# Layer norm's two products of ones one column tile earlier, the sum of its squares on VectorE, and a small sum ahead of a weights' product in the last norm

## The chip, the cores and the metric

The kernel runs on one core of a Trainium2 chip. Its time is the device time of one execution in microseconds (us); a kernel is run several times and the median is given. A profiled execution comes with a trace of every instruction of the core's engines: TensorE (PE, with its weight loads PEld), VectorE (DVE), ScalarE (ACT), GpSimd (POOL) and SyncE (SP). SyncE only issues transfers; ScalarE and GpSimd issue some of theirs too.

## The reference

One block of a streaming encoder, for 512 frames of 1024 channels, in float32. Two mixers read the same normalized input and one projection matrix: a gated delta rule with eight heads (with a short convolution of 4 taps, and an output projection `dn_w_o`), and a convolution of 31 taps with a layer norm behind it. Gates merge the two, `w_out` projects, and a SwiGLU layer and a last RMS norm follow. What the change touches is the layer norm and the last norm:

```python
def layernorm(x, w, b):
    mu = jnp.mean(x32, axis=-1, keepdims=True)
    xc = x32 - mu
    y = xc * lax.rsqrt(jnp.mean(xc * xc, axis=-1, keepdims=True) + EPS)
    return y * w + b

c = causal_depthwise_conv(c, cm_dw_w) + cm_dw_b       # 31 taps
c = silu(layernorm(c, cm_ln_w, cm_ln_b))
out_b = c @ cm_w_pw2 + cm_b_pw2
out_a = o @ dn_w_o
x = x + (gate_a * out_a + gate_b * out_b) @ w_out
...
return rmsnorm(x, norm_f_w)                           # last norm
```

## The kernel before

Large products run in three parts, because each float32 operand is split into a high and a low half of a rounded format: high x high, high x low, low x high (`split3`, L115, product at L121). A piece of weights of 128 x 1024 is fetched by SyncE into `raw` (L108); ScalarE makes `whi` from it (L111), VectorE `wlo` = `raw` - `whi` (L112). Three such pieces exist at once, so a piece can be fetched when `wlo` three pieces before is made, and made when TensorE has finished the piece three before.

Activations lie as channels x frames: eight tiles of 128 x 512. A column tile (`col_tile`, L123) is 8 x 3 = 24 products of 128x512 into one bank of PSUM `mm`, of which there are three. The stage that matters here has two loops over eight column tiles:

- The first loop (from L866) multiplies the delta rule's output (`oh`, `ol`, in the trace `yh`, `yl`) with `dn_w_o`. Each tile is multiplied by its gate on VectorE (L875), which frees the bank. The gate is fetched from DRAM into `gsl` (L854), which has two buffers, so gate j + 2 can be fetched when L875 of tile j is done.
- The second loop (from L884) multiplies the layer norm's output, again split into `yh` and `yl` (`split`, L857, ScalarE at L860 and VectorE at L861), with `cm_w_pw2`.

The layer norm lies inside the first loop. The eight convolved tiles are `cv[0]` to `cv[7]`, their sum over tiles is `sacc`. `ln_mean` (L689) sums `sacc` over the partitions by a product with a matrix of ones (L691), scales it to the mean (L693, ScalarE), subtracts it from the eight tiles (L696, VectorE), squares them (L698 and L701, ScalarE) and adds the squares up (L702, GpSimd). `ln_norm` (L705) sums that by a second product of ones (L707), takes the root (L709, ScalarE) and the reciprocal (L710, VectorE), scales the eight tiles (L712, VectorE) and applies weight, bias and SiLU (L713, ScalarE). The two products of ones stand ahead of column tiles 2 and 5 (counted from 0).

Beside this, sums of weights for later stages are made in the background. Each time a piece of weights is fetched, `fill` (L200) may issue a transfer that adds weights in DRAM (`feed_one`, L186: L192 on SyncE, L196 on GpSimd), or load half of a block of `wdn` into `wsh` (`half_load`, L175; the load is L166 on SyncE), or, for a block loaded before, make four adds on GpSimd (L172) and store them to `wsum` (L173, GpSimd's queue) by `dsums_add` (L168). `wsh` has one buffer, so the next load L166 waits for the store L173. While the flag `norming` is set (from the start of this stage to `ln_norm`) no block is loaded or added. `dsums_add` orders its adds behind the instruction kept in `last[0]`.

A scheduler sets each engine's order of instructions from the order in the program and its own estimate; each engine then works through its own list in order, waiting on semaphores of the others.

The last norm works per 128 frames (`squares`, L1156): the squares of a part of a row are summed into `acc` while they are made (ScalarE L1161 or VectorE L1163), a small add (L1164) brings the parts together, GpSimd raises the sum to the power -1/2 (L1166). `weighted` (L1168, through the helper at L1002) multiplies the row by the norm's weight, `scaled` (L1171; L1174 on ScalarE, L1176 on VectorE) applies the root, and the row is stored (L1181). The very last piece of work, the second half of frames 128 to 255, comes in two quarters of 256 columns.

Of the kernel before, what the change touches and what calls it, by code (L numbers as in the profile page):

```python
# [10 lines left out]
ALU = mybir.AluOpType  # L11
# [17 lines left out]
EPS = 1e-6  # L29
# [3 lines left out]
def block_kernel(ctx, tc, a):  # L33
    nc = tc.nc
    V, S, G, PE = nc.vector, nc.scalar, nc.gpsimd, nc.tensor
# [63 lines left out]
    last = [None]  # L99
# [23 lines left out]
    def col_tile(ps, ap, xh, xl):  # L123
        hi, lo = unit(ap)
        for k in range(KD):
            s = slice(k * P, (k + 1) * P)
            split3(ps, (hi[:, s], lo[:, s]), xh[k], xl[k], k == 0, k == KD - 1)
# [14 lines left out]
    cs = []  # L142
# [69 lines left out]
    with tc.tile_pool(name="st", bufs=2) as st:  # L212
# [56 lines left out]
        for k in range(KD):  # L269
# [3 lines left out]
                                   op0=ALU.mult, op1=ALU.subtract)  # L273
            if k % 2 == 0:
                c = slice(k * P, k * P + 256)
# [66 lines left out]
        for k in range(2, 4):  # L342
# [6 lines left out]
                        in1=ss[:, 1].rearrange("p (n a) -> p n a", a=1).broadcast_to([P, NT, 16]), op=ALU.mult)  # L349
# [6 lines left out]
                        in1=rowp[:, 1:2, :].broadcast_to([P, NT, H]), op=ALU.add)  # L356
# [9 lines left out]
        with tc.issue_after(ln_.ins):  # L366
            for g_ in gated:
# [8 lines left out]
                        op=ALU.mult)  # L376
# [312 lines left out]
    def ln_mean():  # L689
        ps = psm.tile([P, T], F32, name="mm")  # L690
        PE.matmul(ps, ones, sacc, start=True, stop=True)  # L691
        mu = tp.tile([P, T], F32, name="pa", bufs=1)
        S.activation(mu, ps, AF.Copy, scale=1.0 / D)  # L693
        vacc = tp.tile([P, T], F32, name="sacc", bufs=1)
        for i in range(KD):
            V.tensor_tensor(out=cv[i], in0=cv[i], in1=mu, op=ALU.subtract)  # L696
            if i == 0:
                S.activation(vacc, cv[i], AF.Square)  # L698
            else:
                sq2 = tp.tile([P, T], F32, name="acc4")  # L700
                S.activation(sq2, cv[i], AF.Square)  # L701
                last[0] = G.tensor_tensor(out=vacc, in0=vacc, in1=sq2, op=ALU.add)  # L702
        return vacc

    def ln_norm(vacc):  # L705
        ps = psm.tile([P, T], F32, name="mm")
        PE.matmul(ps, ones, vacc, start=True, stop=True)  # L707
        rstd = tp.tile([P, T], F32, name="pa", bufs=1)
        S.activation(rstd, ps, AF.Sqrt, scale=1.0 / D, bias=epsc)  # L709
        V.reciprocal(out=rstd, in_=rstd)  # L710
        for i in range(KD):
            V.tensor_tensor(out=cv[i], in0=cv[i], in1=rstd, op=ALU.mult)  # L712
            S.activation(cv[i], cv[i], AF.Silu, scale=ln_w[:, i:i + 1], bias=ln_b[:, i:i + 1])  # L713
# [138 lines left out]
    def gate_of(i):  # L852
        sg = mp.tile([P, T], F32, name="gsl", bufs=2)
        nc.sync.dma_start(sg, sgd[i])  # L854
        return sg
# [8 lines left out]
    mas = []  # L864
    oh, ol = zip(*[split(zall[:, k, :]) for k in range(KD)])
    for j in range(KD):  # L866
        if j == 2:
            vacc = ln_mean()
        if j == 5:
            ln_norm(vacc)  # L870
            norming[0] = False
        ps = psm.tile([P, T], F32, name="mm")
        col_tile(ps, a["wo"][j], oh, ol)
        ma = mp.tile([P, T], F32, name="ma", bufs=KD + 1)
        V.tensor_tensor(out=ma, in0=ps, in1=gate_of(j), op=ALU.mult)  # L875
        mas.append(ma)
# [124 lines left out]
    def tt(out, in0, in1, op, eng=V):  # L1001
        return eng.tensor_tensor(out=out, in0=in0, in1=in1, op=op)  # L1002
# [153 lines left out]
    def squares(hf, n, cs, last=False, eng=S):  # L1156

        sq, acc = dp.tile([P, T], F32, name="rms_sq", bufs=1)[:, 0:cs.stop - cs.start], ss3[:, hf, n:n + 1]
        y, t = y2[:, n, cs], ss3[:, 2, n:n + 1]
        if eng is S:  # L1160
            S.activation(sq, y, AF.Square, scale=1.0 / 32, accum_out=acc)  # L1161
        else:
            V.scalar_tensor_tensor(out=sq, in0=y, scalar=1.0 / D, in1=y, op0=ALU.mult, op1=ALU.mult, accum_out=acc)  # L1163
        V.tensor_scalar(out=t, in0=acc, scalar1=t if hf else EPS, scalar2=None, op0=ALU.add)  # L1164
        if last:
            G.tensor_tensor(out=ss3[:, 3, n:n + 1], in0=t, in1=half, op=ALU.pow)  # L1166

    def weighted(n, cs, eng=G):  # L1168
        tt(ow[n][:, cs], y2[:, n, cs], nfw[:, cs], ALU.mult, eng)
# [8 lines left out]
    def out(n, c):  # L1178
        for cs, eng, q in ((slice(0, c), S, nc.scalar), (slice(c, D), V, nc.sync)):
            scaled(n, cs, eng)  # L1180
            q.dma_start(a["out"][n][:, cs], ow[n][:, cs])  # L1181

    def add(n, cs, what, op=ALU.add, eng=V):
        tt(y2[:, n, cs], y2[:, n, cs], what, op, eng)
# [84 lines left out]
    def part(k, n, ps, c, cw, first, last):  # L1269
        w, x, j = ws[k // 2], set4[k // 2], k % 2  # L1270
        cs, ts = slice(j * T + c, j * T + c + cw), slice(j * TH + n * P, j * TH + n * P + P)
        split3(ps, (w[0][:, cs], w[1][:, cs]), x[0][:, ts], x[1][:, ts], first, last, mv=True)

    K0 = 2 * (len(ws) - 3)
    for k in range(K0):
        for n in range(2):
            part(k, n, p3[n], 0, T, k == 0, n == 1 and k == K0 - 1)
        if k < 2:
            add(2 + k, c1, p4[k])
            squares(0, 2 + k, c1)  # L1280
            squares(1, 2 + k, c2, True)
            weighted(2 + k, c2)
            add(k, c1, p2[k])
            squares(0, k, c1)
        elif k < 4:
            weighted(k, c1)
            for cs, q in ((c2, nc.sync), (c1, nc.scalar)):
                with behind(mybir.EngineType.Activation):
                    scaled(k, cs, S)
                q.dma_start(a["out"][k][:, cs], ow[k][:, cs])  # L1290
            weighted(k - 2, c1, V)
# [6 lines left out]
    for c, b in ((0, bank), (256, bank2)):  # L1298
        ps = b()[:, c:c + 256]
        for k in range(K0, FK):  # L1300
            part(k, 1, ps, c, 256, k == K0, k == FK - 1)
        cs = slice(T + c, T + c + 256)
        if not c:
            out(0, 384)
        add(1, cs, ps)
        squares(4 if c else 1, 1, cs, c, V if c else S)
        weighted(1, cs, V)
    out(1, 384)


# [56 lines left out]
```

## Time and profile before

| | |
|---|---|
| time, median of 3 runs | 957.11 us (956.86 to 957.43) |
| profiled execution | 957.3 us, span of its trace 955.5 us |
| TensorE busy | 942.1 us (99%) |
| VectorE, ScalarE, GpSimd busy | 729.6, 535.3, 350.4 us |
| granted TensorE clock | 0.998 |
| layer norm's products of ones (L691, L707) | start at 482.80 and 500.02 us |
| second loop's first product | 517.28 us |

A row of a timeline gives start and duration in us, engine, line, operation, tiles written and read, count, and in brackets the idle time of the engine just before, with what ended it. Where an instruction waits for several things, the row names the one that came last by the profile; a transfer may have come later. "SPq" is SyncE's queue. A row of waits gives who waited for whom: us in total, times, longest.

### The profile page before, as it was taken

How to read it: one execution, taken by the hardware profiler on the slowest of the kernel's cores; microseconds unless marked ns; L12 is line 12 of the kernel's file. 1: busy time of each engine (PE TensorE's matmuls, PEld its weight loads, DVE VectorE, ACT ScalarE, POOL GpSimd, SP SyncE). 2: the span in 40 equal slices, each digit the busy share in tenths (PEclk: the TensorE clock that was granted, in tenths of full speed). 3: DMA queues.
4: the chain of work that ended last, by engine and by line, in shares of the span. 5: the costliest groups of instructions: out<-in, count | busy, mean ns of one | idle time of the engine just before them, and what ended most of it. 6: DMA issues, size and time to landing. Idle time of an engine off the chain costs nothing.

```text
span 955.5 us, 14889 instructions
## 1 busy us (share of the span) xinstructions
PE 942.1 (99%) x5208; PEld 794.2 (83%) x5208; DVE 729.6 (76%) x1134; ACT 535.3 (56%) x1102; POOL 350.4 (37%) x555
## 2 busy tenths in 40 slices
PE   9999999999999999999999999999999999999997
PEld 6778888887887888888877888888889999988885
DVE  4999887876888888898877753766425887888896
ACT  7697786969756674634546323323324445456545
POOL 1136434344533447444163432254351111133042
PEclk9999999999999999999999999999999999999999
DMA  9234322233232246979887984598899655578654
GB/s 324 104 128 118 102 82 86 92 99 101 70 92 87 89 133 158 316 223 267 273 274 220 315 235 172 181 264 290 277 255 216 198 188 190 177 228 262 210 178 155
DMA packets 78186, 177.39 MB, mean 186 GB/s; under 512 B 10080, under 2 KB 19472, under 8 KB 77088
## 3 DMA queue, kind: packets, MB, share of 16 engines
q1 hardware_dynamic: 66528, 144.89, 45.5%
q0 software_dynamic: 10288, 28.90, 13.4%
q10 hardware_dynamic: 1296, 2.67, 0.7%
q8 instruction: 41, 0.67, 0.3%
q14 instruction: 33, 0.27, 0.1%
HBM read 156.22 MB, written 45.37 MB: 211 GB/s over the span
## 4 chain that ended last, share of the span: by engine, by line
PE 85%; ACT 3%; DVE 3%; issue 2%; DMA 1%; POOL 1%; POOLq 0%; SPq 0%; ACTq 0%; DVEq 0%
PE mm L121 57%; PE w L121 19%; PE g L437 1%; DMA raw<-s 1%; DVE wlo L112 1%; PE st L616 1%; PE st L610 1%; PE b L542 1%; PE g L470 1%; PE b L548 1%; PE b L566 1%; PE st L604 1%; PE g L519 1%; PE st L615 1%; PE st L605 1%
## 5 line engine op out<-in xcount | busy, mean ns | idle before, releaser
L111 ACT ACTIVATE whi<-raw 128x1024 fp32r<-128x1024 f32 (+1 forms) x191 | 196.2, 1029 | 240.7 <-PE mm L121 143.6
L112 DVE TENSOR_TENSOR wlo<-raw,whi 128x1024 fp32r<-128x1024 f32 (+1 forms) x191 | 240.5, 1260 | 88.0 <-ACT whi L111 87.4
L121 PE MATMUL mm<-hh,whi 128*128 128x512 f32 (+1 forms) x688 | 268.9, 391 | 0.3 <-ACT hh L336 0.3
L121 PE MATMUL mm<-hl,whi 128*128 128x512 f32 (+1 forms) x688 | 264.4, 384 | 0.0
L121 PE MATMUL mm<-hh,wlo 128*128 128x512 f32 (+1 forms) x688 | 263.6, 384 | 0.2 <-DVE wlo L112 0.2
L672 DVE SCALAR_TENSOR_TENSOR cps<-c,c31w,cps 128x512 f32<-128x512 f32 x240 | 180.3, 751 | 6.1 <-ACT cps L670 1.8
L121 PEld LDWEIGHTS mm<-hh,wlo 128*128 128x128 f32 x688 | 129.6, 188 | 23.6 <-DVE wlo L112 0.4
L121 PEld LDWEIGHTS mm<-hh,whi 128*128 128x128 f32 x688 | 129.7, 189 | 22.5 <-ACT hh L336 0.8
L121 PEld LDWEIGHTS mm<-hl,whi 128*128 128x128 f32 x688 | 129.9, 189 | 20.8
L1002 POOL TENSOR_TENSOR fm<-fm 128x256 f32<-128x256 f32 x33 | 28.0, 850 | 111.9 <-DVE s L1002 87.4
L424 DVE SCALAR_TENSOR_TENSOR acc<-mm,c4w,acc 128x511 f32<-128x511 f32 (+2 forms) x72 | 53.1, 741 | 6.1 <-ACT acc L421 5.9
L506 POOL TENSOR_TENSOR ytm<-U,y 128x60 f32<-128x60 f32 (+14 forms) x120 | 37.1, 309 | 48.2 <-DMA U<-sc 39.4
L121 PE MATMUL mm<-yl,whi 128*128 128x512 f32 x128 | 50.0, 391 | 2.3 <-DVE yl L861 2.3
L121 PE MATMUL mm<-yh,whi 128*128 128x512 f32 x128 | 50.7, 396 | 0.0
L121 PE MATMUL mm<-yh,wlo 128*128 128x512 f32 x128 | 49.9, 390 | 0.0
L121 PE MATMUL w<-hh,wlo 128*128 128x256 f32 x168 | 47.7, 284 | 0.3 <-DVE wlo L112 0.3
L121 PE MATMUL w<-hh,whi 128*128 128x256 f32 x168 | 47.6, 284 | 0.0
L121 PE MATMUL w<-hl,whi 128*128 128x256 f32 x168 | 47.5, 283 | 0.0
L121 PE MATMUL w<-wlo,fh 128*128 128x512 f32 (+1 forms) x115 | 44.3, 385 | 0.2 <-DVE wlo L112 0.2
L121 PE MATMUL w<-whi,fh 128*128 128x512 f32 (+1 forms) x115 | 44.2, 385 | 0.0
L121 PE MATMUL w<-whi,fl 128*128 128x512 f32 (+1 forms) x115 | 44.2, 384 | 0.0
L196 POOL DMA_DIRECT2D s<-in_wgu_dram x24 | 23.6, 997 | 47.9 <-DMA s<-in_wgu_dram 47.9
(332 smaller groups left out, 1915.8 us busy)
## 6 DMA issues: line engine op xcount, KB each, us to landing
raw<-in_win_dram SPq DMA_DIRECT2D x61, 512.0 KB, 3.5
raw<-in_wgu_dram SPq DMA_DIRECT2D x32, 512.0 KB, 3.6
s<-in_wgu_dram SPq DMA_DIRECT2D x48, 256.0 KB, 5.3
raw<-s SPq DMA_DIRECT2D x48, 256.0 KB, 3.6
raw<-wsum SPq DMA_DIRECT2D x44, 256.0 KB, 3.8
raw<-in_wdn_dram SPq DMA_DIRECT2D x33, 256.0 KB, 3.5
s<-in_wgu_dram POOLq DMA_DIRECT2D x24, 256.0 KB, 7.2
s<-s POOLq DMA_DIRECT2D x24, 256.0 KB, 7.0
```

Source lines behind the costliest of these rows:

```text
L111: marked(S.activation(hi, raw, AF.Copy), "unit")
L112: marked(V.tensor_tensor(out=lo, in0=raw, in1=hi.bitcast(F32), op=ALU.subtract), "unit")
L121: marked(PE.matmul(ps, l, r, start=first and i == 0, stop=last and i == 2))
L196: fed.append(nc.gpsimd.dma_start(*begun.pop(0), accum_op=ALU.add, max_dma_last_dim=2048))
L424: marked(V.scalar_tensor_tensor(out=acc[:, s:], in0=ps[:, :T - s], scalar=c4w[:, j, k:k + 1], in1=acc[:, s:], op0=ALU.mult, op1=ALU.add))
L437: PE.transpose(ps[:, n, :], src[:, n, :], ident)
L470: PE.matmul(ps[:, n, :], kT[:, n, :], kT[:, n, :], start=True, stop=True)
L506: G.tensor_tensor(out=tm[:, :, 0:w], in0=U[:, k, :, k + 1:], in1=y[:, :, k:k + 1].broadcast_to([P, NT, w]), op=ALU.mult)
L519: PE.matmul(ps[:, n, :], kT[:, n, :], qT[:, n, :], start=True, stop=True)
L542: PE.matmul(ps[:, n, 0:16], Ud[:, n, :], xc[:, n, 0:16], start=True, stop=True)
L672: V.scalar_tensor_tensor(out=acc, in0=c[:, k:k + T], scalar=c31w[:, i, k:k + 1], in1=acc, op0=ALU.mult, op1=ALU.add)
L1002: return eng.tensor_tensor(out=out, in0=in0, in1=in1, op=op)
```

## The change

`ln_mean` is called ahead of column tile 1 instead of 2, `ln_norm` ahead of 4 instead of 5. The adds of the squares (L702) go from GpSimd to VectorE, and are no longer kept in `last[0]`. In the last norm `squares` returns its small add, and in the last two quarters `weighted` is issued behind it.

```diff
@@ ln_mean
                 sq2 = tp.tile([P, T], F32, name="acc4")
                 S.activation(sq2, cv[i], AF.Square)
-                last[0] = G.tensor_tensor(out=vacc, in0=vacc, in1=sq2, op=ALU.add)
+                V.tensor_tensor(out=vacc, in0=vacc, in1=sq2, op=ALU.add)
         return vacc
@@ first loop
     for j in range(KD):
-        if j == 2:
+        if j == 1:
             vacc = ln_mean()
-        if j == 5:
+        if j == 4:
             ln_norm(vacc)
             norming[0] = False
@@ squares
-        V.tensor_scalar(out=t, in0=acc, scalar1=t if hf else EPS, scalar2=None, op0=ALU.add)
+        s_ = V.tensor_scalar(out=t, in0=acc, scalar1=t if hf else EPS, scalar2=None, op0=ALU.add)
         if last:
             G.tensor_tensor(out=ss3[:, 3, n:n + 1], in0=t, in1=half, op=ALU.pow)
+        return s_
@@ last two quarters
         add(1, cs, ps)
-        squares(4 if c else 1, 1, cs, c, V if c else S)
-        weighted(1, cs, V)
+        s_ = squares(4 if c else 1, 1, cs, c, V if c else S)
+        with tc.issue_after(s_.ins):
+            weighted(1, cs, V)
```

Behind the diff the lines of the last norm have numbers one to three higher (L1176 becomes L1177).

The scheduler moves more than these lines. First, VectorE in the first half of the layer norm (`acc_...` are the squares, L875 the gate products of tiles 1 and 2), a piece of the difference:

```order
+L702 TENSOR_TENSOR sacc<-sacc,acc_5219 128x512
 L875 TENSOR_TENSOR ma<-mm,gsl 128x512
-L112 TENSOR_TENSOR wlo<-raw,whi 128x1024
-L696 TENSOR_TENSOR cv<-cv,pa 128x512 x8
-L875 TENSOR_TENSOR ma<-mm,gsl 128x512
-L112 TENSOR_TENSOR wlo<-raw,whi 128x1024
+L702 TENSOR_TENSOR sacc<-sacc,acc_5223 128x512
+L112 TENSOR_TENSOR wlo<-raw,whi 128x1024
+L702 TENSOR_TENSOR sacc<-sacc,acc_5227 128x512
```

The seven adds stand between the subtractions L696 and among the gate products and weights' halves, where before the eight subtractions stood in one row. At the same place GpSimd's list, where the end of the seven adds and the background adds stood:

```order
-L702 TENSOR_TENSOR sacc<-sacc,acc_5258 128x512
-L702 TENSOR_TENSOR sacc<-sacc,acc_5262 128x512
-L172 TENSOR_TENSOR wsh<-wsh 128x256 x4
-L173 DMA wsum<-wsh 512x1x256
+L172 TENSOR_TENSOR wsh<-wsh 128x256 x4
+L173 DMA wsum<-wsh 512x1x256
+L196 DMA s_128<-s_126 128x512
 L196 DMA s_127<-in_wgu_dram 128x512
 L172 TENSOR_TENSOR wsh<-wsh 128x256 x4
```

The first four background adds and their store no longer stand behind the adds of the squares, and go ahead of one transfer. Second, the end of the first loop: VectorE from the scaling of the eight tiles to the first gate product of the second loop, before,

```order
L712 TENSOR_TENSOR cv<-cv,pa 128x512 x8
L875 TENSOR_TENSOR ma<-mm,gsl 128x512
L112 TENSOR_TENSOR wlo<-raw,whi 128x1024
L861 TENSOR_TENSOR yl<-cv,yh 128x512 x4
L875 TENSOR_TENSOR ma<-mm,gsl 128x512
L861 TENSOR_TENSOR yl<-cv,yh 128x512 x4
L112 TENSOR_TENSOR wlo<-raw,whi 128x1024 x2
```

and now:

```order
L712 TENSOR_TENSOR cv<-cv,pa 128x512 x8
L875 TENSOR_TENSOR ma<-mm,gsl 128x512
L112 TENSOR_TENSOR wlo<-raw,whi 128x1024 x2
L875 TENSOR_TENSOR ma<-mm,gsl 128x512
L112 TENSOR_TENSOR wlo<-raw,whi 128x1024
L861 TENSOR_TENSOR yl<-cv,yh 128x512 x6
L875 TENSOR_TENSOR ma<-mm,gsl 128x512
L861 TENSOR_TENSOR yl<-cv,yh 128x512
L112 TENSOR_TENSOR wlo<-raw,whi 128x1024
L861 TENSOR_TENSOR yl<-cv,yh 128x512
```

The gate products are those of tiles 6 and 7 before, 5, 6 and 7 now; the first L112 was that of the second loop's first tile, and is now that of tile 7. ScalarE at the same place:

```order
 L713 ACT_TABLE_LOAD
 L713 ACTIVATE cv<-cv,vec 128x512 x8
-L860 ACTIVATE yh<-cv 128x512 x8
-L111 ACTIVATE whi<-raw 128x1024 x3
+L111 ACTIVATE whi<-raw 128x1024 x2
+L860 ACTIVATE yh<-cv 128x512 x7
+L111 ACTIVATE whi<-raw 128x1024
+L860 ACTIVATE yh<-cv 128x512
+L111 ACTIVATE whi<-raw 128x1024
```

Two weight tiles now stand ahead of `yh`, and a third ahead of its last tile. Third, VectorE in the last norm, from the scaling of the row of frames 0 to 127:

```order
-L1176 TENSOR_SCALAR ow_8763<-ow_8763,ss_8762 128x640
+L1177 TENSOR_SCALAR ow_8763<-ow_8763,ss_8762 128x640
+L1164 TENSOR_SCALAR ss_8762<-ss_8762 128x1
 L1002 TENSOR_TENSOR ow_8764<-y_8761,nfw 128x256
-L1164 TENSOR_SCALAR ss_8762<-ss_8762 128x1
 L1002 TENSOR_TENSOR y_8761<-y_8761,mm 128x256
 L1163 SCALAR_TENSOR_TENSOR rms_sq,ss_8762<-y_8761 128x256
+L1164 TENSOR_SCALAR ss_8762<-ss_8762 128x1
 L1002 TENSOR_TENSOR ow_8764<-y_8761,nfw 128x256
-L1164 TENSOR_SCALAR ss_8762<-ss_8762 128x1
-L1176 TENSOR_SCALAR ow_8764<-ow_8764,ss_8762 128x640
+L1177 TENSOR_SCALAR ow_8764<-ow_8764,ss_8762 128x640
```

In both quarters the small add L1164 now stands ahead of the weights' product (`ow<-y,nfw`); between the row's scaling and the add of the second quarter's product (`y<-y,mm`) the same two instructions stand, the other way round.

## The prediction, made before the changed kernel ran

> **What bounds the kernel now.** I read the page first, then TensorE's waits, then the timeline around the longest of them.
>
> ```profile
> span 955.5 us, 14889 instructions
> PE 942.1 (99%) x5208; PEld 794.2 (83%) x5208; DVE 729.6 (76%) x1134; ACT 535.3 (56%) x1102; POOL 350.4 (37%) x555
> ```
>
> ```profile
> PE mm L121 <- DVE yl L861: 2.3, 1, 2.3
> ...
> PE w L121 <- DVE wlo L112: 0.5, 2, 0.3
> ```
>
> TensorE is busy 942.1 of 955.5 us, so only what shortens its few waits or the tail can shorten the kernel. In the second fence (who waited for whom: us in total, times, longest) the longest wait is one of 2.3 us for `yl`, the low half of the layer norm's output. The timeline of TensorE (start, duration, engine, line, tiles) shows where it stands:
>
> ```profile
> 477.36 0.39 PE L121 MATMUL mm<-yh,whi 128*128 128x512 f32 x1
> ...
> 482.80 1.02 PE L691 MATMUL mm<-sacc,cst 128*128 128x512 f32 x2
> ...
> 500.02 1.08 PE L707 MATMUL mm<-sacc,cst 128*128 128x512 f32 x2
> ...
> 511.84 0.39 PE L121 MATMUL mm<-yh,whi 128*128 128x512 f32 x1
> ...
> 517.28 0.39 PE L121 MATMUL mm<-yh,whi 128*128 128x512 f32 x1
> 519.94 0.50 PE L121 MATMUL mm<-yl,whi 128*128 128x512 f32 x1 [2.28 <-DVE yl L861]
> ...
> 525.61 0.39 PE L121 MATMUL mm<-yh,whi 128*128 128x512 f32 x1
> ...
> 544.65 0.39 PE L121 MATMUL mm<-yh,whi 128*128 128x512 f32 x1
> ```
>
> These are first products of column tiles of 24. From 525.61 to 544.65 there are 84 products: 0.2267 us each, 5.44 a tile. The tile that begins at 517.28 takes 8.33 us to 525.61, so the wait and the slower products behind it cost 8.33 - 5.44 = **2.89 us**. The product of ones with its slower neighbour costs (500.02 - 482.80) - 72 x 0.2267 = 0.90 us. Now VectorE's timeline at that place:
>
> ```profile
> 507.20 4.90 DVE L712 TENSOR_TENSOR cv<-cv,pa 128x512 f32<-128x512 f32 x8
> 517.46 0.69 DVE L875 TENSOR_TENSOR ma<-mm,gsl 128x512 f32<-128x512 f32 x1 [5.36 <-PE mm L121]
> ```
>
> VectorE finished L712 at 512.1 and stood still for 5.36 us ahead of the gate product of tile 6 (L875); an L112 and then `yl` (L861) queue behind it. The row blames a matmul, but tile 6 had ended at 511.84, where tile 7 begins. SyncE's timeline, its waits and the landing times of the gate loads (`gsl`) tell more:
>
> ```profile
> 497.54 0.53 SPq L854 DMA_DIRECT2D gsl<-sgd  x1
> ...
> 507.48 0.60 SPq L166 DMA_DIRECT2D wsh<-in_wdn_dram  x1
> ...
> 509.39 0.53 SPq L854 DMA_DIRECT2D gsl<-sgd  x1
> ```
>
> ```profile
> SPq L166 <- DMA wsum<-wsh: 14.5, 3, 9.3
> ...
> SPq L854 <- DMA gsl<-sgd: 5.8, 1, 5.8
> ...
> DMA to landing us min/median/max: 3.3/6.3/8.1
> ```
>
> The gate load of tile 6 was issued at 509.39. Two gate loads later SyncE itself needed it landed and waited 5.8 us, from the load it issued at about 511.5 to 517.4. That is eight microseconds after the issue, like the longest of these landings, and when it had landed L875 began. It was issued so late because SyncE had stood from 498.1 to 507.48 at L166, 9.3 us, for the store of L173. GpSimd's timeline:
>
> ```profile
> 487.05 12.88 POOL L702 TENSOR_TENSOR sacc<-sacc,acc 128x512 f32<-128x512 f32 x7 [0.37 <-ACT acc L701]
> 499.89 4.04 POOL L172 TENSOR_TENSOR wsh<-wsh 128x256 f32<-128x256 f32 x4
> 504.23 0.80 POOL L173 DMA_DIRECT2D wsum<-wsh  x1 [0.31 <-POOL wsh L172]
> ```
>
> L173 follows L172, and L172, whose data had long landed, stands in GpSimd's queue behind the seven adds of the squares L702, which end at 499.9. So the 2.89 us of TensorE start on GpSimd: L702, L172, L173, L166, the gate load, L875, `yl`.
>
> **The change part by part.** *Products of ones one tile earlier, sums on VectorE.* The first now stands at 477.36, the second 17.22 us later at 494.58, and the second loop still starts at 477.36 + 2 x 0.90 + 7 x 5.44 = 517.2, since the same products run. What must be on time, from the timelines of SyncE, VectorE and ScalarE:
>
> ```profile
> 476.01 0.60 SPq L166 DMA_DIRECT2D wsh<-in_wdn_dram  x1
> ...
> 474.98 0.68 DVE L678 TENSOR_TENSOR sacc<-sacc,cv 128x512 f32<-128x512 f32 x1
> ...
> 485.01 9.29 DVE L696 TENSOR_TENSOR cv<-cv,pa 128x512 f32<-128x512 f32 x8
> ...
> 503.09 3.35 DVE L710 RECIPROCAL pa<-pa 128x512 f32<-128x512 f32 x1 [0.58 <-ACT pa L709]
> ...
> 514.42 4.26 ACT L860 ACTIVATE yh<-cv 128x512 fp32r<-128x512 f32 x8
> ```
>
> (a) The first product's sum L678 ends at 475.7, 1.7 us early: no wait.
>
> (b) The squares' sum. L696 starts 2.21 us behind the product of ones (485.01 - 482.80), so at 479.57. VectorE then runs 8 L696 and 7 L702 at 4.90/8 = 0.61 us, one L875 (0.69) and one L112 (1.22): 11.1 us, done at 490.7, 3.9 us ahead of 494.58. Against it stands GpSimd: eight L696 took 9.29 us beside four L702, the same shape alone (L712) 4.90, so one 128x512 add beside it costs VectorE 1.1 us. Without L702 ahead of them, the four L172 of half that width start when their load (issued 476.01) has landed, about 482. They cost between 0 and 4 x 1.1 = 4.4 us; I take 3, nearer their own 4.04/4: done at 493.7, no wait. At the upper bound it is 495.1, a wait of 0.5.
>
> [...]
>
> (c) The second half. L710 began 3.07 us after L707, so 497.65, unless the gate load of tile 3, issued after L875 of tile 1 (490 to 491), holds VectorE: landing in 3.3 to 8.1 us, it allows L710 between 497.65 and 501. I take 499 (the median 6.3). L710 ends at 502.4, L875 of tile 4 at 503, L712 (4.90 and 0 to 4.4 for the second four L172, here 2.3, as some run beside L710) at 510.3, L875 of tile 5 and then L112, tile 7's low half of weights, at 512.1. This L112 stood ahead of the reciprocal before; now it stands behind L712. TensorE reaches its third product of tile 7 at 511.8 + 0.45 = 512.25. So it is just in time; with everything early it is ready at 508.6, with everything late (L710 at 501, 4.4 us for the four L172) at 516.1. I book **0.2 us**, between 0 and 3.9.
>
> (d) `yh` and `yl`. ScalarE now makes two weight tiles ahead of L860; the second waits for tile 6 to end (511.8), so L860 starts at 512.9 (514.42 before) at 0.53 each. VectorE follows with L875 of tile 6, one L112 and six L861 from about 514.5 at 0.62 each: the first is ready at 515.1, the loop needs it at 517.5 and then one per 0.68 us. The last two stand behind the gate product of tile 7 and an L112, ready near 521 against 522.3. The gate load of tile 6 is now issued when L875 of tile 4 frees its buffer, about 503, and lands by 511.2. SyncE's L166 is reached near 496, and its store, issued near 488, has landed by then. So the **-2.89 us** goes.
>
> *The last norm.* The small sum L1164 is put ahead of the weights' product. The end of TensorE's and of VectorE's timeline:
>
> ```profile
> 948.08 0.28 PE L121 MATMUL mm<-wlo,fh 128*128 128x256 f32 x1
> ...
> 947.63 0.42 DVE L1002 TENSOR_TENSOR ow<-y,nfw 128x256 f32<-128x256 f32 x1
> 948.22 0.21 DVE L1164 TENSOR_SCALAR ss<-ss 128x1 f32<-128x1 f32 x1 [0.16 <-ACT rms_sq L1161]
> 948.40 0.42 DVE L1002 TENSOR_TENSOR y<-y,mm 128x256 f32<-128x256 f32 x1
> ...
> 949.20 0.08 DVE L1163 DVE_READ_ACCUMULATOR rms_sq<-y 128x1 f32 x1
> 949.20 0.42 DVE L1002 TENSOR_TENSOR ow<-y,nfw 128x256 f32<-128x256 f32 x1
> 949.54 0.20 DVE L1164 TENSOR_SCALAR ss<-ss 128x1 f32<-128x1 f32 x1
> ```
>
> For the last quarter this removes the product between 949.20 and 949.54 from the way: -0.34, of which 0.1 stays as the wait for the accumulator (read until 949.28). But for the quarter before, the same order makes the product wait for ScalarE's squares: it moves from 947.63, where it filled an idle gap, to behind L1164 at 948.40, and pushes the last add from 948.40 to 948.74, as its product ended at 948.36. That is +0.34. Sum +0.1, between -0.25 (if the push were hidden) and +0.34: **+0.12 us**. The power on GpSimd, the scaling and both stores follow as before.
>
> **Sum.** -2.89 + 0.2 + 0.12 = -2.57 us. The profiled execution took 957.3 us for its span of 955.5, 0.2 above the median of 957.11: 954.7 for it, 957.11 - 2.57 = **954.5** for the median. In the later stages the products into `w` wait 0.5 us in all (the second row of TensorE's waits), so I see nothing that gives the time back.
>
> **Rivals.** 0.2% of 957.11, about what a measurement can tell from no change, is 1.9 us: faster is below 955.2, slower above 959.0.
>
> *Tile 7's low half of weights comes late* (c): a new wait of 0.9 to 3.9 us in place of the old, 957.11 - 2.77 + the wait: 955.2 to 958.2. For it: both slow bounds add up on one engine. Against it: they must coincide. Chance 0.18.
>
> *The old wait stays*, another gate load or store holding SyncE or VectorE as before: +0.12, 957.2. For it: landings up to 8.1 us with loads more crowded, as L172 and its stores move to where tiles and gates load. Against it: the chain through L702 is gone, and (d) leaves 2.4 us for the first `yl`. Chance 0.09.
>
> *Slower: VectorE becomes the bound at the second product of ones.*
>
> ```profile
> 484.00:495.00 11.00, 11.00 (x50) 9.09 (x49) 11.00 (x11) 5.78 (x9) 8.44 (x6) 1.00 0.86 268
> ```
>
> VectorE (third pair after the stretch's length) was busy for all of 484 to 495, and the change gives it seven adds more. From 479.57, less 1.9 for the two others, fifteen operations have 13.1 us, 0.87 each; above that TensorE waits, and above 1.19 each the wait exceeds 4.7 us and the kernel is over 959.0. At the 9.29/8 = 1.16 us of the old L696 the wait is 4.3 and the time 958.6; at 1.71, the pace beside an unbroken row of GpSimd adds ((9.29 - 4 x 0.61)/4), it is 12.6 and the time 966.9. Against it: what slowed L696 was L702 itself, which is gone, and four half-wide adds stand in its place. Chance 0.06.
>
> [...]
>
> **How the numbers follow.** Forecast 0.67, rivals 0.18, 0.09 and 0.06. Faster 0.67; same 0.18 + 0.09 = 0.27; slower 0.06. The forecast's own range is 953.9 (nothing booked in (c), a tail gain) to 955.2. To leave no more than 2 in 10 out I take 953.8 to 957.2.
>
> **What would show it.** TensorE's waits no longer list `yl` L861 at 2.3 us, and the second loop's first tile takes 5.5 us; L707 follows L691 by 17.2 us; one L696 takes 0.7 to 0.9 us on average instead of 9.29/8 = 1.16; the four L172 run near 482 and SyncE passes L166 by 497. Wrong at (c): TensorE waits for `wlo` L112 in tile 7. Wrong at (b): L707 waits for `sacc` L702. Wrong in the tail: from the last matmul to the last L1164 is not about 0.1 us longer than 949.54 - 948.08.

## The result and the profile after

| kernel | median of its runs | lowest to highest | kernel before beside it | ratio, 95% interval |
|---|---|---|---|---|
| changed kernel, first measurement | 954.28 us | 953.07 to 954.67 us | 956.22 us, 954.14 to 957.43 | 0.9978 (0.9968 to 0.9988) |
| changed kernel, second measurement | 954.41 us | 953.87 to 955.77 us | 955.96 us, 954.33 to 959.04 | 0.9981 (0.9971 to 0.9990) |

The changed kernel is faster by 0.22% (0.12 to 0.32%), some 2.1 us; the second measurement says 0.19%. The forecast was 954.5 us, inside the range of 953.8 to 957.2. The kernel before is now near 956 us rather than the 957.11 of its first three runs, and its times spread far more than the changed kernel's. The first experiment below shows why, for three executions. One execution of the changed kernel in the first measurement ran at a granted clock of 0.85 and took 1030.99 us; it is left out of the table.

The page of the changed kernel (from the second measurement; its execution took 954.42 us), and TensorE's waits (who waited for whom: us in total, times, longest):

```profile
span 952.5 us, 14885 instructions
...
PE 941.3 (99%) x5208; PEld 793.5 (83%) x5208; DVE 732.0 (77%) x1141; ACT 535.9 (56%) x1102; POOL 351.0 (37%) x548
```

```profile
PE g L258 <- DVE epsc L73: 1.0, 1, 1.0
...
PE w L121 <- DVE wlo L112: 0.5, 2, 0.3
```

No wait for `yl` is left: the longest is one of 1.0 us at the start of the kernel, which was there before, and the 0.5 us for `wlo` are those of the later stage, as before. TensorE's timeline, the two products of ones and the first product of the second loop's first and second tile:

```profile
477.33 1.02 PE L691 MATMUL mm<-sacc,cst 128*128 128x512 f32 x2
...
494.55 1.02 PE L707 MATMUL mm<-sacc,cst 128*128 128x512 f32 x2
...
517.21 0.39 PE L121 MATMUL mm<-yh,whi 128*128 128x512 f32 x1
...
522.65 0.39 PE L121 MATMUL mm<-yh,whi 128*128 128x512 f32 x1
```

L707 follows L691 by 17.22 us, and the second loop starts at 517.21 (517.28 before), both as worked out. Its first tile takes 5.44 us instead of 8.33: the 2.89 us are gone to the last hundredth. VectorE's timeline of the same stage:

```profile
479.54 2.49 DVE L696 TENSOR_TENSOR cv<-cv,pa 128x512 f32<-128x512 f32 x4
481.95 0.69 DVE L702 TENSOR_TENSOR sacc<-sacc,acc 128x512 f32<-128x512 f32 x1
...
487.36 0.69 DVE L875 TENSOR_TENSOR ma<-mm,gsl 128x512 f32<-128x512 f32 x1
...
489.70 0.69 DVE L702 TENSOR_TENSOR sacc<-sacc,acc 128x512 f32<-128x512 f32 x1
490.30 0.69 DVE L875 TENSOR_TENSOR ma<-mm,gsl 128x512 f32<-128x512 f32 x1
...
497.61 3.35 DVE L710 RECIPROCAL pa<-pa 128x512 f32<-128x512 f32 x1 [0.78 <-ACT pa L709]
...
501.70 4.89 DVE L712 TENSOR_TENSOR cv<-cv,pa 128x512 f32<-128x512 f32 x8
...
507.14 1.22 DVE L112 TENSOR_TENSOR wlo<-raw,whi 128x1024 fp32r<-128x1024 f32 x1
...
514.03 3.69 DVE L861 TENSOR_TENSOR yl<-cv,yh 128x512 fp32r<-128x512 f32 x6
```

The eight subtractions and the seven adds, with one gate product and one L112 among them, start 0.6 us apart; the squares' sum is complete at 490.39, 4.2 us ahead of its product. The first `yl` begins at 514.03 and is ready near 514.7, some 2.7 us ahead of the product that needs it. GpSimd's and SyncE's timelines there, and SyncE's waits at L166:

```profile
482.64 10.89 POOL L172 TENSOR_TENSOR wsh<-wsh 128x256 f32<-128x256 f32 x4 [0.31 <-DMA wsh<-in_wdn_dram]
493.83 0.80 POOL L173 DMA_DIRECT2D wsum<-wsh  x1 [0.30 <-POOL wsh L172]
```

```profile
498.83 0.60 SPq L166 DMA_DIRECT2D wsh<-in_wdn_dram  x1
...
501.81 0.33 SPq L854 DMA_DIRECT2D gsl<-sgd  x1
```

```profile
SPq L166 <- DMA wsum<-wsh: 8.9, 4, 5.8
```

The four background adds start at 482.64 instead of 499.89, but take 10.89 us instead of 4.04. Their store is issued at 493.83 (504.23 before), SyncE still stands 5.8 us at L166 and passes it at 498.8 (507.48 before), and the gate load of tile 6 is issued at 501.81, 7.6 us earlier than before.

### The profile page after: what moved, and what is told of

Its sections match the earlier page's. It is cut to its first block, busy times and chain, and to the rows that moved or that the text cites. A ratio compares the mean times of both kernels' runs of the same rounds, so it can differ in the third digit from the quotient of the medians.

```text
span 1028.9 us, 14885 instructions
## 1 busy us (share of the span) xinstructions
PE 1020.2 (99%) x5208; PEld 823.9 (80%) x5208; DVE 729.5 (71%) x1141; ACT 538.4 (52%) x1102; POOL 334.9 (33%) x548
## 4 chain that ended last, share of the span: by engine, by line
PE 98%; DMA 0%; DVE 0%; ACT 0%; issue 0%; SPq 0%; POOLq 0%; POOL 0%; DVEq 0%
PE mm L121 64%; PE w L121 22%; PE g L437 1%; PE st L616 1%; PE g L470 1%; PE st L610 1%; PE g L519 1%; PE b L542 1%; PE b L548 1%; PE b L121 1%; PE st L615 1%; PE b L566 1%; PE st L605 1%; PE st L604 1%; PE b L586 0%; PE b L591 0%
## 5 line engine op out<-in xcount | busy, mean ns | idle before, releaser
L112 DVE TENSOR_TENSOR wlo<-raw,whi 128x1024 fp32r<-128x1024 f32 (+1 forms) x191 | 235.2, 1232 | 117.3 <-ACT whi L111 116.1
L121 PE MATMUL mm<-hh,whi 128*128 128x512 f32 (+1 forms) x688 | 285.3, 415 | 0.0
L121 PE MATMUL mm<-hl,whi 128*128 128x512 f32 (+1 forms) x688 | 281.1, 409 | 0.0
L121 PE MATMUL mm<-hh,wlo 128*128 128x512 f32 (+1 forms) x688 | 279.6, 407 | 0.0
L121 PEld LDWEIGHTS mm<-hh,whi 128*128 128x128 f32 x688 | 133.0, 193 | 30.7 <-issue 0.2
L121 PEld LDWEIGHTS mm<-hl,whi 128*128 128x128 f32 x688 | 133.2, 194 | 29.8
L121 PE MATMUL mm<-yh,whi 128*128 128x512 f32 x128 | 54.2, 423 | 0.0
L121 PE MATMUL mm<-yl,whi 128*128 128x512 f32 x128 | 53.5, 418 | 0.0
L121 PE MATMUL mm<-yh,wlo 128*128 128x512 f32 x128 | 53.2, 416 | 0.0
L506 POOL TENSOR_TENSOR ytm<-U,y 128x60 f32<-128x60 f32 (+14 forms) x120 | 32.9, 274 | 45.1 <-DMA U<-sc 36.3
```

Source lines behind the costliest of these rows:

```text
L112: marked(V.tensor_tensor(out=lo, in0=raw, in1=hi.bitcast(F32), op=ALU.subtract), "unit")
L121: marked(PE.matmul(ps, l, r, start=first and i == 0, stop=last and i == 2))
L506: G.tensor_tensor(out=tm[:, :, 0:w], in0=U[:, k, :, k + 1:], in1=y[:, :, k:k + 1].broadcast_to([P, NT, w]), op=ALU.mult)
```

## The experiments

**How long is the stall of the kernel before?** Two more profiles of it, unchanged.

> The kernel before, unchanged, another execution's profile, to see how large the stall is when it isn't the one execution that the prediction was worked out from. If the 2.89 us are a fixed property of the order: the second loop's first tile takes 8.3 us again. If the stall is only as long as the gate load of tile 6 happens to take (landings of 3.3 to 8.1 us): it differs, between 0.5 and 3 us, which would make the usual gain smaller than 2.89.

> As the run before it: a third execution's profile of the kernel before. Fixed property: 8.3 us for the second loop's first tile; landing time: another value between 5.9 and 8.5 us.

The first took 955.01 us, the second 958.68. TensorE at the second loop's first tile, and VectorE's gate product of tile 6, in the first:

```profile
517.30 0.39 PE L121 MATMUL mm<-yh,whi 128*128 128x512 f32 x1
518.22 0.50 PE L121 MATMUL mm<-yl,whi 128*128 128x512 f32 x1 [0.53 <-DVE yl L861]
...
523.84 0.39 PE L121 MATMUL mm<-yh,whi 128*128 128x512 f32 x1
```

```profile
515.74 0.69 DVE L875 TENSOR_TENSOR ma<-mm,gsl 128x512 f32<-128x512 f32 x1 [3.62 <-DMA gsl<-sgd]
```

Here the row itself names the gate load: it was issued at 509.39 as before, and its gate product could start 6.35 us later instead of 8.07. The tile takes 6.54 us, an excess of 1.10 over 5.44. In the second execution, TensorE's timeline, and the busy time by stretch (after the length: PE, PEld, DVE, ACT, POOL, then the granted clock, DMA share and GB/s):

```profile
517.66 0.39 PE L121 MATMUL mm<-yh,whi 128*128 128x512 f32 x1
520.31 0.50 PE L121 MATMUL mm<-yl,whi 128*128 128x512 f32 x1 [2.26 <-DVE yl L861]
...
522.68 0.63 PE L121 MATMUL mm<-yh,whi 128*128 128x512 f32 x1
...
527.31 0.39 PE L121 MATMUL mm<-yh,whi 128*128 128x512 f32 x1
```

```profile
521.50:522.00 0.50, 0.50 (x4) 0.39 (x3) 0.50 (x2) 0.00 (x0) 0.00 (x0) 0.78 1.43 275
522.00:523.00 1.00, 1.00 (x4) 0.81 (x3) 1.00 (x3) 0.00 (x0) 0.00 (x0) 0.50 1.01 129
...
525.00:525.50 0.50, 0.50 (x4) 0.38 (x3) 0.50 (x2) 0.00 (x0) 0.00 (x0) 0.81 1.02 350
```

The wait is 2.26 us, as long as in the execution of the prediction, but products behind it ran at a granted clock of 0.50 for some 3.4 us (an estimate: the means of 0.78 and 0.81, read as mixtures of the 1.00 and 0.50 of the stretches around them, put its begin near 521.8 and its end near 525.2), and the tile takes 9.65 us: an excess of 4.21. So the stall is not a fixed size: 2.89, 1.10 and 4.21 us in three executions. Each one's time less its excess is 957.3 - 2.89 = 954.4, 955.01 - 1.10 = 953.9 and 958.68 - 4.21 = 954.5: in these three the stall makes the spread, and without it each lies where the changed kernel lies. The kernel's other executions have no trace, so that the stall spreads them too is not shown. The expectation of 5.9 to 8.5 us for the tile left the clock out, and missed it.

**Only the adds of the squares on VectorE**, the products of ones left where they were.

```diff
-                last[0] = G.tensor_tensor(out=vacc, in0=vacc, in1=sq2, op=ALU.add)
+                V.tensor_tensor(out=vacc, in0=vacc, in1=sq2, op=ALU.add)
```

> Of the change only the adds of the squares on VectorE; the products of ones stay ahead of tiles 2 and 5. If the stall comes from L172 queued behind the seven L702 on GpSimd: the four L172 run near 482 instead of 499.9, L166 is passed before 498, the gate load of tile 6 is issued when its buffer is free, near 508 (tile 4's L875 stands behind L710), and lands by 516; the stall of 2.89 goes in most part: 954.2 to 955.5, with a wait of 0 to 0.5 us of L707 for the squares' sum (done 496 to 500.5 against 500.02). If it is the place of the products of ones that counts (the end of the first loop too crowded when L712 ends at 512.1): the stall stays, 957 +- 0.5.

954.03 us, ratio 0.9973 (0.9964 to 0.9983); the second loop's first tile takes 5.44 us. GpSimd and SyncE:

```profile
482.73 4.36 POOL L172 TENSOR_TENSOR wsh<-wsh 128x256 f32<-128x256 f32 x4 [0.23 <-DMA wsh<-in_wdn_dram]
```

```profile
498.80 0.60 SPq L166 DMA_DIRECT2D wsh<-in_wdn_dram  x1
...
500.88 0.33 SPq L854 DMA_DIRECT2D gsl<-sgd  x1
```

The adds run at 482.73 as expected. Their store, issued at 487.39, lands 7.8 us later, and SyncE waits for it no more: L166 comes at 498.80, a little later than the 498 expected, only because it stands behind the gate load of tile 5 (497.83), which waits for L875 of tile 3. The gate load of tile 6 is issued at 500.88, as soon as L875 of tile 4 (500.16) has freed its buffer. The expectation had it near 508, since it put that L875 behind L710; it ran ahead of it. The stall goes without any move of the products of ones.

**Only the products of ones one tile earlier**, the adds of the squares left on GpSimd.

```diff
-        if j == 2:
+        if j == 1:
             vacc = ln_mean()
-        if j == 5:
+        if j == 4:
```

> Of the change only the products of ones one tile earlier; L702 stays on GpSimd. L172 then still stands behind the seven L702, but all of it 5.44 us earlier: L702 done near 494.5, L166 passed near 502, gate load of tile 6 issued near 503 to 504, landed by 512. If the late gate load is the cause: the stall goes here too, -2.9, 954.2; L702's end, which lies 0.1 us ahead of L707 now as before, may cost up to 0.5. If the stall needs L702 off GpSimd: 957. If VectorE's order at the loop's end (L112 of tile 7 behind L712) costs: a wait for `wlo`, 955 to 958.

954.53 us, ratio 0.9979 (0.9970 to 0.9989); first tile 5.44 us. GpSimd, SyncE's gate loads of tiles 6 and 7 (one row), and the wait that this adds on TensorE:

```profile
495.00 4.16 POOL L172 TENSOR_TENSOR wsh<-wsh 128x256 f32<-128x256 f32 x4
499.46 0.80 POOL L173 DMA_DIRECT2D wsum<-wsh  x1 [0.30 <-POOL wsh L172]
```

```profile
505.13 4.30 SPq L854 DMA_DIRECT2D gsl<-sgd  x2
```

```profile
PE mm L707 <- POOL sacc L702: 0.3, 1, 0.3
```

The whole chain is there but 4.8 us earlier (L173 at 499.46 instead of 504.23; the gate load of tile 6 at 505.13 instead of 509.39), and that is enough. The squares' sum on GpSimd is now 0.3 us late for L707. Either half of the change removes the stall by itself; together they gain nothing more, save those 0.3 us.

**Three gate buffers instead of two**, nothing of the change.

```diff
-    mp.tile([P, PAD], F32, name="pad", bufs=1)
+    mp.tile([P, PAD - 32], F32, name="pad", bufs=1)
...
-        sg = mp.tile([P, T], F32, name="gsl", bufs=2)
+        sg = mp.tile([P, T], F32, name="gsl", bufs=3)
```

> The kernel before with three buffers for the gates (`gsl`) instead of two, nothing of the change: each gate load can be issued one tile earlier, so that of tile 6 stands in SyncE's list ahead of the L166 that waits 9.3 us, or is issued well before 509. L172, L173 and L166 stay where they were. If the gate load that came late is what held L875, `yl` and TensorE: the stall of 2.89 us goes, 954.2, second loop's first tile 5.5 us, without any change to the layer norm. If VectorE stood for something else (the matmul that the row names, or ScalarE): 957.1, no change.

957.31 us, ratio 1.0005 (0.9996 to 1.0015): by its time the cause was refuted. Its trace says otherwise. No wait for `yl` is left, L875 of tile 6 starts at 513.68, and L166 still waits 9.7 us. But the products of the whole stage are slower. Two of them, 90 products apart:

```profile
530.22 0.40 PE L121 MATMUL mm<-yh,whi 128*128 128x512 f32 x1
...
551.12 0.40 PE L121 MATMUL mm<-yh,whi 128*128 128x512 f32 x1
```

20.90 / 90 = 0.2322 us each, against 0.2267. The stall had gone and the pace had taken as much; two more experiments part them.

**The tiles moved, still two buffers.**

```diff
-    mp.tile([P, PAD], F32, name="pad", bufs=1)
+    mp.tile([P, PAD + 480], F32, name="pad", bufs=1)
```

> The kernel before with the empty tile ahead of this stage's tiles 480 elements (1920 bytes per partition) longer, so that `yh`, `yl` and the tiles behind `gsl` lie where they lay with three gate buffers; still two gate buffers, same order of instructions. If the slower products there (0.2325 us instead of 0.2267) come from where the tiles lie: 0.2325 here too, some 3 us more over this stage's products, with the stall still there: about 959. If they come from the gate loads running earlier: 0.2267 and no change, 956.

958.71 us, ratio 1.0026 (1.0013 to 1.0040). The same two rows:

```profile
529.81 0.40 PE L121 MATMUL mm<-yh,whi 128*128 128x512 f32 x1
...
550.71 0.40 PE L121 MATMUL mm<-yh,whi 128*128 128x512 f32 x1
```

Again 0.2322 us, with two gate buffers as in the kernel before and the stall still there (TensorE waits 0.8 us for `yl`): the pace changed with where the stage's tiles lie in SBUF, not with the number of buffers.

**Three gate buffers, the tiles moved by 512 bytes.**

```diff
-    mp.tile([P, PAD], F32, name="pad", bufs=1)
+    mp.tile([P, PAD - 384], F32, name="pad", bufs=1)
...
-        sg = mp.tile([P, T], F32, name="gsl", bufs=2)
+        sg = mp.tile([P, T], F32, name="gsl", bufs=3)
```

> Three gate buffers again, nothing of the change, but with the empty tile ahead cut by 384 elements, so that the tiles behind `gsl` move by 512 bytes per partition (2048 - 1536) instead of 1920. If the late gate load is the cause of the stall and the products' pace hangs on where the tiles lie within some 512 bytes: products at 0.2267 us, no stall, 954. If any move slows the products: 0.2325 us and 957.

953.86 us, ratio 0.9982 (0.9965 to 0.9998). The same two products, SyncE's waits at L166, and VectorE's gate product of tile 6 with the first `yl`:

```profile
530.21 0.39 PE L121 MATMUL mm<-yh,whi 128*128 128x512 f32 x1
...
550.61 0.39 PE L121 MATMUL mm<-yh,whi 128*128 128x512 f32 x1
```

```profile
SPq L166 <- DMA wsum<-wsh: 40.2, 5, 9.4
```

```profile
511.37 0.69 DVE L875 TENSOR_TENSOR ma<-mm,gsl 128x512 f32<-128x512 f32 x1
514.39 3.67 DVE L861 TENSOR_TENSOR yl<-cv,yh 128x512 fp32r<-128x512 f32 x4 [1.20 <-ACT yh L860]
```

The pace is back at 20.40 / 90 = 0.2267 us, the wait at L166 is as long as ever (9.4 us), and the stall is gone because the gate load of tile 6 no longer stands behind it (it is issued at 496.84, ahead of L166 at 506.79).

**One gate load on another queue.** The cleanest form: no tile moves, the layer norm is that of before.

```diff
-        nc.sync.dma_start(sg, sgd[i])
+        (nc.scalar if i == 6 else nc.sync).dma_start(sg, sgd[i])
```

> The kernel before with one transfer moved: the gate load of tile 6 (L854) is issued by ScalarE, ahead of the root L709, instead of by SyncE behind L166. Nothing of the layer norm is changed and no tile moves in memory. If the late gate load alone holds L875, `yl` and TensorE: it is issued near 501, when L875 of tile 4 frees its buffer, landed before 509.5, and the stall of 2.89 us goes although L166 still waits 9 us: 954 to 955, products at 0.2267 us. If the stall has another cause: 956 to 957, the second loop's first tile 8.3 us.

954.77 us, ratio 0.9984 (0.9972 to 0.9996), first tile 5.44 us. ScalarE's issue of that load, and the wait that stays on SyncE:

```profile
501.67 0.33 ACTq L854 DMA_DIRECT2D gsl<-sgd  x1
```

```profile
SPq L166 <- DMA wsum<-wsh: 32.9, 5, 9.3
```

With one transfer issued at 501.67 instead of 509.39 the stall goes, though L702, L172, L173 and L166 stand as before. The late gate load is the cause, by two experiments, this one and the last, that leave the rest of the chain as it was.

**The tail: only the last quarter reordered**, in the changed kernel.

```diff
-        with tc.issue_after(s_.ins):
+        with tc.issue_after(s_.ins) if c else nullcontext():
             weighted(1, cs, V)
```

> The changed kernel, but in the last norm only the last quarter's weights' product is put behind the small sum; the quarter before keeps its order of before. By the prediction's sum the last quarter alone gains: its product no longer stands between the squares and L1164, while the product before it stays in the idle gap. From the last matmul's start to the end of the last L1164 1.42 to 1.46 us, against 1.73 with both quarters changed and 1.67 before; with the 0.1 us more that GpSimd's power took beside VectorE's product in the changed kernel, 0.2 to 0.3 us shorter than the changed kernel in all. If the push of the first quarter costs nothing: no difference to the changed kernel.

953.97 us, ratio 0.9978 (0.9966 to 0.9991), no difference from the changed kernel that times can tell; the trace can. The last matmul starts at 944.86 in the changed kernel and at 944.56 here. VectorE's and GpSimd's end of the changed kernel, and VectorE's here:

```profile
944.99 0.21 DVE L1164 TENSOR_SCALAR ss<-ss 128x1 f32<-128x1 f32 x1 [0.49 <-ACT rms_sq L1161]
945.12 0.42 DVE L1002 TENSOR_TENSOR ow<-y,nfw 128x256 f32<-128x256 f32 x1
945.46 0.42 DVE L1002 TENSOR_TENSOR y<-y,mm 128x256 f32<-128x256 f32 x1
...
946.38 0.21 DVE L1164 TENSOR_SCALAR ss<-ss 128x1 f32<-128x1 f32 x1
```

```profile
946.67 0.66 POOL L1166 TENSOR_TENSOR ss<-ss,half 128x1 f32<-128x1 f32 x1 [2.76 <-DVE ss L1164]
```

```profile
944.88 0.42 DVE L1002 TENSOR_TENSOR y<-y,mm 128x256 f32<-128x256 f32 x1
...
945.81 0.21 DVE L1164 TENSOR_SCALAR ss<-ss 128x1 f32<-128x1 f32 x1
```

From the last matmul to the end of the last L1164 it is 946.59 - 944.86 = 1.73 us in the changed kernel and 946.02 - 944.56 = 1.46 here, 0.27 shorter as expected (949.74 - 948.08 = 1.66 before). So the quarter before does better in its old order.

**The adds on VectorE and the last quarter, no earlier products of ones.** The edits of the first and of the last experiment on the kernel before.

> The adds of the squares on VectorE, the products of ones left ahead of tiles 2 and 5, and only the last quarter of the last norm reordered. If the stall needs no earlier products of ones and the tail is as argued, the best of both: the stall gone as with the adds alone, the tail 0.1 us shorter than before instead of 0.17 longer; 953.8 to 954.2 against the changed kernel's 954.4. If the earlier products of ones help: not below the changed kernel.

954.00 us, ratio 0.9976 (0.9966 to 0.9987). Its second loop's first tile takes 5.44 us and its tail is 1.45 us, so by its trace it has the best of both; by its time it is not below the changed kernel by an amount that can be told.

## Why the prediction was right, and where it was not

- **What bounds the kernel.** The chain was read rightly to its end, also against the row that blamed a matmul: two experiments that leave L702, L172, L173 and L166 in place and issue the gate load of tile 6 earlier take the stall away, and one profile names the load in the row itself.
- **Its price, 2.89 us,** was the mis-sized term. It was read from one execution and stood against a median of three runs, all long (956.86 to 957.43). Three profiled executions have 2.89, 1.10 and 4.21 us. The forecast of 954.5 for the changed kernel holds, since all the stall went whatever its size, and in part by luck: the three runs and the execution with 2.89 us were long ones alike. From the 956.22 of all ten runs the same sum gives 953.65, below its own range, against 954.28 measured. The gain of 2.57 us against the kernel before is nearer 2.1 (1.1 to 3.1); of the three traces one has a shorter stall, of 1.10 us. The landings of 3.3 to 8.1 us that were quoted were reason enough to give it a range: from its issue to its gate product the load of tile 6 took 8.07 us in that execution and 6.35 in the next.
- **(a)** The sum of the first product was in time (no wait of L691).
- **(b)** Right in its outcome, wrong in the loser. I booked 3 us on VectorE for the four L172; VectorE lost nothing (490.39 where the sum without contention said 490.7), and GpSimd lost 10.89 - 4.04 = 6.9. With that the store was issued at 493.83 rather than near 488, and the sign "SyncE passes L166 by 497" failed: 498.8, 5.8 us of waiting. It cost nothing, as the gate load of tile 6 was still issued 7.6 us earlier. The sign "one L696 takes 0.7 to 0.9 us" failed too, as VectorE lost nothing: they start 0.6 us apart. That VectorE would be the one to lose was my estimate from the 4.4 us that L696 lost beside L702; which engine loses beside L172, that row did not show.
- **(c)** L710 started at 497.61, the early end of 497.65 to 501, and L712 took 4.89 us, none lost. Tile 7's `wlo` was ready at 508.36 (early end 508.6) against a need of 512.2: the booked 0.2 us was 0, and the rival of 0.18 did not come near.
- **(d)** Right: first `yl` at 514.03 (about 514.5 in the sum), and the two behind the gate product of tile 7 in time.
- **The tail** was booked at +0.12 us. The last L1164 ends 0.07 us later after the last matmul, for the reason given (the first quarter's product pushed the last add). A second piece was missed: the power L1166 took 0.66 us instead of 0.55, with VectorE's moved product now running beside it (0.66 in the two runs with only the last quarter moved, too). Together +0.17 at the start of the last scaling (2.50 us behind the last matmul instead of 2.33); with the last quarter alone, 0.27 less.
- **The other rivals.** The old wait did not stay. VectorE did not become the bound: its fifteen operations and two others took 10.85 us from 479.54, and 4.2 us were to spare.

## What to carry to other kernels

A wait that follows a transfer had no fixed size here (an excess of 2.89, 1.10 and 4.21 us in three executions): take such a wait from several executions before it enters a sum, and look at the engine's clock behind it (0.50 from 522 to 525 in one of the three). Where one queue carries both urgent and background transfers, look for the background one whose wait stands ahead; issuing the urgent load from another queue, or one buffer earlier, did as much here as moving the arithmetic (ratios to the kernel before of 0.9984 and 0.9982, against 0.9981). And the experiment that added a buffer also moved its neighbours in memory, and each product took 0.2322 us instead of 0.2267: read the products' pace before the time of such an experiment is believed.

## What the runs showed that was not expected

**The products' pace changed with the place of the tiles.** With the tiles of this stage 1920 bytes further in each partition, each product took 0.2322 us instead of 0.2267, 2.4% more, whether a third buffer was there or not; 512 bytes further it was 0.2267. The granted clock was 1.00 from 480 to 560 in all three, so the clock is not the reason. In time it was about the 3 us by which 958.71 stands above 955.76. Why is not known; one move that harms and one that doesn't give no rule.

**Behind one stall of 2.26 us the clock was at half.** In that execution the granted clock was 0.50 from 522 to 525; in another, after a wait of 2.28 us, it was 1.00 in every stretch from 517 to 526. Two equal waits had unequal ends, and what parts them no run here shows.

**Beside a row of VectorE's operations one GpSimd add took 5.40 us.** In the kernel before, L696 (487.42, 489.12, 490.82) and GpSimd's L702 (487.05, 488.73, 490.42) started by turns, one each in some 1.7 us, and VectorE lost 9.29 - 4.90 = 4.4 us. In the changed kernel GpSimd's first two L172, one by one, were these:

```profile
482.64 5.40 POOL L172 TENSOR_TENSOR wsh<-wsh 128x256 f32<-128x256 f32 x1 [0.31 <-DMA wsh<-in_wdn_dram]
...
488.12 2.86 POOL L172 TENSOR_TENSOR wsh<-wsh 128x256 f32<-128x256 f32 x1
```

The last of the four took 0.74 us. While the first ran, from 482.64 to 488.04, VectorE went without a gap from L702 and L696 into the gate product of 487.36, which ended at 488.05; the second ended at 490.98, and the next gate product at 490.99. So both ended within 0.01 us of the end of a gate product; why, no run here shows.

Which of the two engines lost was not the same in all runs. The eight L696 of the kernel before took 9.29, 9.98 and 8.41 us in its three traced executions. With the tiles moved and two gate buffers they took 4.91, and GpSimd's first L702 3.15 instead of 1.6; with the same move and three buffers they took 9.30 again. With only the adds on VectorE, the four L172 met an L112 and the first four L696 and both engines lost: these took 1.54 and 3.58 us instead of 1.22 and 2.49, the L172 4.36 instead of 4.04. What decides it, no run here tells.
